# A diffusion backbone layer: row tiles of the modulation scaled on ScalarE and added up in SBUF by transfers, transposes emitted later

## The chip, the core and the metric

The kernel runs on one core of a Trainium2 chip. The metric is device time in microseconds (us). Three runs of the kernel before took 2056.44, 2061.23 and 2062.34 us, so the median is 2061.23.

## The reference

One layer of a hybrid diffusion backbone over 256 latent tokens and 256 context tokens, width 2048, all in float32:

- `mod = silu(c) @ w_mod + b_mod` gives six vectors of 2048: shift, scale and gate for the mixer (parts 0, 1, 2) and for the ConvFFN (parts 3, 4, 5). The context's own vector `c_ctx` needs parts 0 and 1 only.
- `h = rms_norm(x) * g * (1 + scale) + shift`, then one input projection `h @ w_in` (2048 x 13344) feeds windowed attention (16 query heads, 4 key heads, QK-norm, rotary, sinks, context keys) and a gated linear attention (GLA, 4 heads, both directions).
- Both are projected to 2048, weighted by sigmoid gates, added, projected again, and `x = x + gate * y`.
- ConvFFN: `h2 @ w_up` (2048 x 11264), a depthwise convolution of width 3, `silu(a) * g`, `@ w_down`, and `x = x + gate * y`. Only the latent stream is returned.

## The kernel before, in words

**The arithmetic.** Each float32 matrix is taken as two float32r halves: `hi` is a rounded copy made on ScalarE (L61), `lo` the rest, made on VectorE (L62). A product is then three on TensorE: hi by hi, hi by lo, lo by hi (L163 to L165, L186 to L189).

**Chunks.** Weights stream in chunks of two row tiles by 512 columns, 512 KB, loaded by SyncE's queue into four `raw` buffers (L68, `wload`, L137), split into three pairs `whi`, `wlo` (`wsplit`, L143). `proj_nat` (L152) sums 12 products of 512 columns into each of two or four PSUM banks' tiles for a chunk, `proj_T` (L169) does the same with the weights as the stationary side. Over a whole row range of 2048 there are 8 chunks. At the end `evac` takes the banks.

**Background.** Before each chunk `tick` (L124) may emit a step of `beside` (the generator of the GLA's or the attention's own work) and of the list `bg_steps`, at paces set in the program: so many steps a chunk. A Tile scheduler then orders each engine's instructions; an engine runs its own list strictly in order, and a transfer waits on the queue of the engine that issues it.

**The modulation.** Parts 0 and 1 are made on TensorE at the start, in five groups of row tiles, between loads of the tokens (`mod_both`, L196). Parts 3, 4, 2 and 5 belong to the latent stream alone and are background (`mod_latent`, L225): 128 steps, each loading a 256 x 512 piece of `w_mod` into one of the four `raw` buffers and doing two VectorE instructions `macc = raw * ccol + macc` over 128x512 (L237, L239). After 16 row tiles, `macc` is summed over the partitions (transposed in 32x32 blocks, reduced, one small product, L243 to L254). The paces are 0.7 a chunk beside the GLA, 2.0 beside the keys and values, 0 beside the queries, 0.5 after.

**Stages in order.** Start: tokens, parts 0 and 1, and for each group of row tiles its share of the first four projections. Then the low-rank decay input (L433), GLA heads 0 to 3 beside the other key and value projections, keys and values of attention (KA, VA), four query blocks with attention beside the next (L702), the gated GLA output (RB, L784), the merge (GA, attn_o, GB, gla_o for four column blocks, L799 to L823), the output projection (L838), then up and down projections of the ConvFFN in two halves.

**Transposes.** Results that must become a stationary side are transposed on TensorE against `ident`, four 128x128 products each, directly in `evac`: `ptk` (L680) after the key norm, `ptq` (L696), `pto` (L779, `to_T`) for the gated output and the merge, `ptx1` (L846).

**Queues.** SyncE issues the weights; GpSimd issues small parameters (`lm`, `wtm`, `wlr`, L408 to L426, the attention mask, L638), clears the GLA's `segs` (L466) and adds `gc` (L482).

Of the kernel before, what the change touches and what calls it, by code (L numbers as in the profile page):

```python
# [8 lines left out]
F32 = mybir.dt.float32  # L9
# [7 lines left out]
P = 128  # L17
D = 2048
# [12 lines left out]
def layer_kernel(ctx, tc, A, out):  # L31
# [16 lines left out]
    F2_BUFS = {"fa": 4, "fb": 4, "fc": 6, "mod": 2}  # L48
# [53 lines left out]
    def columns(name, parts, eng=G):  # L102
        rows = W2("mod", "rows", [P, P])
# [48 lines left out]
    def proj_nat(w, r0, c0, kts, lhs, evac):  # L152
        """out[token, feature] for 512 features; lhs[tile](kt) -> (hi, lo) [K, 128]"""
# [15 lines left out]
    def proj_T(w, c0, kts, rhs, evac):  # L169
        """out[feature, token] for 512 features; rhs: list of f(kt) -> (hi, lo) [K, 256]"""  # L170
# [25 lines left out]
    def mod_both(part, t0, n, dst):  # L196
        """steps for c and c_ctx on the tensor engine; dst[p, c, kt] for kt = t0..t0+n-1"""
# [27 lines left out]
    def mod_latent(part, j, dst):  # L225
        """steps for c alone: products summed over the row tiles on the vector engine"""
        a = []
        c0 = part * D + j * 512

        def step(k0):  # L230
            if k0 == 0:
                a.append(W2("mod", "macc", [P, 512]))
            raw = wload(w_mod[k0 * P:k0 * P + 256, c0:c0 + 512])
            for k in range(2):
                kt = k0 + k
                if kt == 0:
                    V.tensor_scalar(a[0], raw[:, 0, :], ccol[:, 0:1], None, op0=ALU.mult)  # L237
                else:
                    V.scalar_tensor_tensor(a[0], raw[:, k, :], ccol[:, kt:kt + 1], a[0],  # L239
                                           op0=ALU.mult, op1=ALU.add)  # L240
            if k0 == KT - 2:
                tr = W2("mod", "mtr", [P, 16, 32])
                V.transpose(tr.rearrange("p a c -> p (a c)"), a[0])  # L243
                rs = sm.tile([P, 16], F32, name="mrs", tag="mrs", bufs=2)
                V.tensor_reduce(rs, tr, op=ALU.add, axis=AX.X)
                pc = bank("pcl", (32, 16))
                PE.matmul(pc, sel[:, 0:32], rs, start=True, stop=True)
                pv = pc.rearrange("p (a b) -> p b a", b=4)
                d = dst[:, 4 * j:4 * j + 4]
                for b4 in range(4):  # L250
                    V.tensor_copy(d[32 * b4:32 * b4 + 32, :], pv[:, b4, :])
                b0 = part * 16 + j * 4
                V.tensor_tensor(d, d, bmod[:, b0:b0 + 4], op=ALU.add)

        return [lambda k0=k0: step(k0) for k0 in range(0, KT, 2)]
# [20 lines left out]
    def rms_scale(ss, n, shape):  # L276
        """(ss / n + eps) ** -0.5: exp(-ln / 2) with a Newton step"""
# [12 lines left out]
    def token_rows(tag, name, cols):  # L290
        """one factor a token, [P, 1] per tile of tokens, as a row in every partition"""
# [51 lines left out]
    def affine_split(hi, lo, xk, row, scale, shift):  # L343
        """halves of xk * row * scale + shift; xk is overwritten"""
# [12 lines left out]
    # with each part of h, that part of the sums of four projections  # L357
# [102 lines left out]
    def gla_A(h, kb, qb, res):  # L460
# [81 lines left out]
        # context keys: decay to the end (forward) or to the start (backward) of the context  # L542
# [110 lines left out]
    def norm_rope(b, r, t):  # L653
        """normalise four heads of 128 and rotate; returns [P, 4, 128] in SBUF"""
# [21 lines left out]
    def ka_evac(i, b):  # L676
        z = norm_rope(b, rk if i < 2 else None, i % 2)
        pt = bank("ptk", (P, 4, P))
        for h in range(4):
            PE.transpose(pt[:, h, :], z[:, h, :], ident)  # L680
        split(kTh[:, :, i * P:(i + 1) * P], kTl[:, :, i * P:(i + 1) * P], pt)

    bg_rate[0] = 2.0
# [5 lines left out]
    def qa_block(g):  # L689
        qT = M("qT", [P, 2, 4, T], F32R)  # L690

        def evac(t, b):
            z = norm_rope(b, rq, t)
            pt = bank("ptq", (P, 4, P))
            for h in range(4):
                PE.transpose(pt[:, h, :], z[:, h, :], ident)  # L696
            split(qT[:, 0, :, t * P:(t + 1) * P], qT[:, 1, :, t * P:(t + 1) * P], pt)
# [63 lines left out]
    for g in range(4):  # L761
        beside[:] = [attend(g, qTs), 0.8, 0.0]
# [6 lines left out]
    bg_rate[0] = 0.5  # L769
# [13 lines left out]
    for j in range(4):  # L783
        def rb_evac(t, b, j=j):  # L784
# [5 lines left out]
            to_T(s_, gh, gl, j, t)  # L790
# [11 lines left out]
    for j in range(4):  # L802
# [15 lines left out]
        def mg_evac(t, b, j=j, a1=a1, a2=a2):  # L818
            V.tensor_tensor(a2[t], b, a2[t], op=ALU.mult)
            V.tensor_tensor(a2[t], a2[t], a1[t], op=ALU.add)  # L820
            to_T(a2[t], mh, ml, j, t)
# [7 lines left out]
    while bg_steps:  # L829
        bg_steps.pop(0)()  # L830
# [6 lines left out]
    for j in range(4):  # L837
        def wo_evac(t, b, j=j):  # L838
# [5 lines left out]
            pt = bank("ptx1", (P, 4, P), side=True)  # L844
            for k in range(4):
                PE.transpose(pt[:, k, :], x1[t][:, j * 512 + k * P:j * 512 + (k + 1) * P], ident)  # L846
            dst = x1T[j // 2][:, (j % 2) * 4:(j % 2) * 4 + 4, t * P:(t + 1) * P]
            S.activation(dst, pt, AF.Copy)
# [109 lines left out]
```

## Time and profile before

| what | value |
|---|---|
| median of three runs | 2061.23 us |
| profiled execution, its span | 2061.8 us |
| instructions | 30115 |
| HBM read | 409.63 MB |
| queue of SyncE | 406.89 MB, 63.3% of 16 DMA engines' span |
| queue of GpSimd | 4.74 MB, 0.8% |

No other time of the profiled execution is listed; its span stands among the three runs. In the rows of the profile `out<-in` gives the tiles, `x` a count; a group's row ends with its busy time, the mean of one in ns, and the idle time of its engine just before it with what ended it. A stretch's row begins with its ends in us.

### The profile page before, as it was taken

The numbers are of one execution on the slowest core, as the hardware profiler recorded it, in microseconds if no ns is written. First come the engines' busy times: TensorE is split into PE (matmuls) and PEld (weight loads), VectorE is DVE, ScalarE is ACT, GpSimd is POOL, SyncE is SP. The second block draws the span as 40 slices with busy tenths as digits, with TensorE's granted clock in tenths as the row PEclk, the third lists the DMA queues.
The fourth block names the chain that finished last, engine by engine and source line by source line (L and its number), as shares of the span: only waits on it lengthen the run. The fifth ranks groups of instructions, "written<-read, shape, count | busy, mean of one in ns | idle before, by whom it ended". The sixth has DMA issues, their size and how long they took to land.

```text
span 2061.8 us, 30115 instructions
## 1 busy us (share of the span) xinstructions
PE 1999.2 (97%) x11792; PEld 1721.8 (84%) x11792; DVE 1405.7 (68%) x2149; ACT 937.4 (45%) x1306; POOL 41.9 (2%) x62
## 2 busy tenths in 40 slices
PE   6899999999999999999999999899999999999999
PEld 4679888888787777777787788899999889999987
DVE  4666778978867888777767665666666555666654
ACT  3323464552346665443334344554455334445533
POOL 0001100001000000000000000000000000000000
PEclk8999999999999999999999999999999999999999
DMA  9976434347664466787888875566666566666664
GB/s 347 337 247 197 120 111 123 113 118 226 213 186 114 121 194 192 254 270 260 264 279 272 294 235 184 164 184 184 184 183 184 194 193 187 184 184 183 183 209 150
DMA packets 214350, 413.71 MB, mean 201 GB/s; under 512 B 12548, under 2 KB 21092, under 8 KB 213184
## 3 DMA queue, kind: packets, MB, share of 16 engines
q1 hardware_dynamic: 212320, 406.89, 63.3%
q0 software_dynamic: 1360, 4.74, 0.8%
q8 instruction: 92, 1.51, 0.3%
q14 instruction: 50, 0.41, 0.1%
q10 hardware_dynamic: 528, 0.17, 0.0%
HBM read 409.63 MB, written 2.11 MB: 200 GB/s over the span
## 4 chain that ended last, share of the span: by engine, by line
PE 60%; issue 18%; DMA 11%; DVE 8%; ACT 2%; POOL 0%; DVEq 0%; ACTq 0%; POOLq 0%
PE acc L189 10%; PE acc L186 10%; PE acc L188 10%; PE acc L165 8%; PE acc L164 8%; PE acc L163 8%; DMA raw<-in_w_mod 8%; DVE wlo L62 3%; DVE macc L239 2%; DMA raw<-in_w_in 2%; PE pm L210 1%; PE pa L503 1%; ACT whi L61 1%; DMA raw<-in_w_gla_o 1%; PE po L589 1%
## 5 line engine op out<-in xcount | busy, mean ns | idle before, releaser
L61 ACT ACTIVATE whi<-raw 128x1024 fp32r<-128x1024 f32 x568 | 601.4, 1059 | 863.7 <-PE acc L165 366.4
L62 DVE TENSOR_TENSOR wlo<-raw,whi 128x1024 fp32r<-128x1024 f32 x568 | 693.3, 1222 | 428.3 <-ACT whi L61 422.7
L186 PE MATMUL acc<-h2h,whi 128*128 128x256 f32 x1408 | 399.5, 284 | 1.3 <-ACT h2h L346 1.3
L188 PE MATMUL acc<-h2l,whi 128*128 128x256 f32 x1408 | 399.5, 284 | 0.0
L189 PE MATMUL acc<-h2h,wlo 128*128 128x256 f32 x1408 | 399.2, 284 | 0.0
L186 PEld LDWEIGHTS acc<-h2h,whi 128*128 128x128 f32 x1408 | 271.3, 193 | 1.9 <-ACT h2h L346 1.8
L188 PEld LDWEIGHTS acc<-h2l,whi 128*128 128x128 f32 x1408 | 271.3, 193 | 0.2
L189 PEld LDWEIGHTS acc<-h2h,wlo 128*128 128x128 f32 x1408 | 271.3, 193 | 0.0
L239 DVE SCALAR_TENSOR_TENSOR macc<-raw,ccol,macc 128x512 f32<-128x512 f32 x240 | 180.6, 752 | 100.5 <-DMA raw<-in_w_mod 97.2
L163 PE MATMUL acc<-whi,h01hi 128*128 128x512 f32 x352 | 139.5, 396 | 0.9 <-ACT whi L61 0.9
L164 PE MATMUL acc<-wlo,h01hi 128*128 128x512 f32 x352 | 139.1, 395 | 1.3 <-DVE wlo L62 1.2
L163 PE MATMUL acc<-whi,h00hi 128*128 128x512 f32 x352 | 139.2, 395 | 0.0
L164 PE MATMUL acc<-wlo,h00hi 128*128 128x512 f32 x352 | 139.0, 395 | 0.2 <-DVE wlo L62 0.2
L165 PE MATMUL acc<-whi,h00lo 128*128 128x512 f32 x352 | 138.6, 394 | 0.0
L165 PE MATMUL acc<-whi,h01lo 128*128 128x512 f32 x352 | 138.2, 392 | 0.0
L163 PE MATMUL acc<-whi,ah 128*128 128x512 f32 x352 | 137.0, 389 | 0.0
L164 PE MATMUL acc<-wlo,ah 128*128 128x512 f32 x352 | 137.0, 389 | 0.0
L165 PE MATMUL acc<-whi,al 128*128 128x512 f32 x352 | 136.9, 389 | 0.0
L164 PEld LDWEIGHTS acc<-wlo,h01hi 128*128 128x128 f32 x352 | 66.4, 189 | 16.0 <-DVE wlo L62 3.2
L163 PEld LDWEIGHTS acc<-whi,h01hi 128*128 128x128 f32 x352 | 66.4, 189 | 14.3 <-ACT whi L61 1.3
L164 PEld LDWEIGHTS acc<-wlo,h00hi 128*128 128x128 f32 x352 | 66.2, 188 | 14.1 <-DVE wlo L62 1.3
L165 PEld LDWEIGHTS acc<-whi,al 128*128 128x128 f32 x352 | 66.1, 188 | 13.8
(369 smaller groups left out, 3393.2 us busy)
## 6 DMA issues: line engine op xcount, KB each, us to landing
raw<-in_w_in SPq DMA_DIRECT2D x208, 512.0 KB, 4.2
raw<-in_w_up SPq DMA_DIRECT2D x176, 512.0 KB, 3.7
raw<-in_w_mod SPq DMA_DIRECT2D x128, 512.0 KB, 3.9
raw<-in_w_down SPq DMA_DIRECT2D x88, 512.0 KB, 3.8
mraw<-in_w_mod SPq DMA_DIRECT2D x32, 1024.0 KB, 10.2
raw<-in_w_attn_o SPq DMA_DIRECT2D x32, 512.0 KB, 4.8
raw<-in_w_gla_o SPq DMA_DIRECT2D x32, 512.0 KB, 5.2
raw<-in_w_out SPq DMA_DIRECT2D x32, 512.0 KB, 3.8
```

Source lines behind the costliest of these rows:

```text
L61: S.activation(hi, src, AF.Copy)
L62: V.tensor_tensor(lo, src, hi.bitcast(F32), op=ALU.subtract)
L163: PE.matmul(banks[i], ahi, hi[:, k, :], start=(kt == kts[0]), stop=False)
L164: PE.matmul(banks[i], ahi, lo[:, k, :], start=False, stop=False)
L165: PE.matmul(banks[i], alo, hi[:, k, :], start=False, stop=(kt == kts[-1]))
L186: PE.matmul(o, whi, ahi, start=(kt == kts[0] and b == 0), stop=False, skip_group_check=True)
L188: PE.matmul(o, whi, alo, start=False, stop=False, skip_group_check=True)
L189: PE.matmul(o, wlo, ahi, start=False, stop=(kt == kts[-1]), skip_group_check=True)
L210: PE.matmul(a[0][q:q + 32, :], cS[:, kt, :], raw[:, k, :], start=(kt < 4), stop=(kt >= 12))
L239: V.scalar_tensor_tensor(a[0], raw[:, k, :], ccol[:, kt:kt + 1], a[0], op0=ALU.mult, op1=ALU.add)
L503: PE.matmul(pa[:, t, :], k2[:, dt, t * P:(t + 1) * P], q2[:, dt, tq * P:(tq + 1) * P], start=(dt == 0), stop=(dt == 1))
L589: PE.matmul(po, x_, y_[:, s, :], start=(n == 0), stop=(n == 11))
```

## The change

Every step of `mod_latent` now covers one row tile by 1024 columns (512 KB as before, 128 steps as before). The tile is loaded by GpSimd's queue into one of two buffers of its own (`mraw2`). ScalarE multiplies it in place by its column of `silu(c)` (for the first row tile, into `macc`), and GpSimd issues a transfer from `mraw2` to `macc`, SBUF to SBUF, that adds. The load for step i+2 is emitted right behind it. Part 5 is emitted beside the first half of the up projection instead of before the output projection. Transposes are put into a list and emitted one to three ticks later. The paces change, and the space reserved for GpSimd's descriptors is set to 4096.

```
-    F2_BUFS = {"fa": 4, "fb": 4, "fc": 6, "mod": 2}
+    F2_BUFS = {"fa": 4, "fb": 4, "fc": 6, "macc": 2, "mraw": 2}
...
-        rows = W2("mod", "rows", [P, P])
+        rows = sm.tile([P, P], F32, name="rows", tag="t128", bufs=2)
...
+    later = []
+    def defer(n, fn):
+        later.append([n, fn])
+    def flush():
+        while later:
+            later.pop(0)[1]()
     def tick():
+        for e in later:
+            e[0] -= 1
+        while later and later[0][0] < 0:
+            later.pop(0)[1]()
...
-    def mod_latent(part, j, dst):
...
-            raw = wload(w_mod[k0 * P:k0 * P + 256, c0:c0 + 512])
-            for k in range(2):
-                kt = k0 + k
-                if kt == 0:
-                    V.tensor_scalar(a[0], raw[:, 0, :], ccol[:, 0:1], None, op0=ALU.mult)
-                else:
-                    V.scalar_tensor_tensor(a[0], raw[:, k, :], ccol[:, kt:kt + 1], a[0],
-                                           op0=ALU.mult, op1=ALU.add)
...
+    def mod_latent(parts):
+        seq = [(part, dst, j, kt) for part, dst in parts for j in range(2) for kt in range(KT)]
+        raws, a = {}, [None]
+        def get(i):
+            if i < len(seq):
+                part, _, j, kt = seq[i]
+                c0 = part * D + j * 1024
+                raws[i] = W2("mraw", "mraw2", [P, 1024])
+                G.dma_start(raws[i], w_mod[kt * P:(kt + 1) * P, c0:c0 + 1024])
...
+        def step(i):
+            part, dst, j, kt = seq[i]
+            if i == 0:
+                get(0)
+                get(1)
+            raw = raws.pop(i)
+            if kt == 0:
+                a[0] = W2("macc", "macc", [P, 1024])
+                S.activation(a[0], raw, AF.Copy, scale=ccol[:, 0:1])
+            else:
+                S.activation(raw, raw, AF.Copy, scale=ccol[:, kt:kt + 1])
+                G.dma_start(a[0], raw, accum_op=ALU.add)
+            get(i + 2)
+            if kt == KT - 1:
+                defer(2, lambda acc=a[0]: finish(part, dst, j, acc))
...
-    for part, dst in ((3, shift2), (4, scale2), (2, gcol1), (5, gcol2)):
-        for j in range(4):
-            bg_steps.extend(mod_latent(part, j, dst))
-    bg_rate[:] = [0.7, 0.0]
+    bg_steps.extend(mod_latent(((3, shift2), (4, scale2), (2, gcol1))))
+    bg_rate[:] = [0.5, 0.0]
...
         z = norm_rope(b, rk if i < 2 else None, i % 2)
-        pt = bank("ptk", (P, 4, P))
-        for h in range(4):
-            PE.transpose(pt[:, h, :], z[:, h, :], ident)
-        split(kTh[:, :, i * P:(i + 1) * P], kTl[:, :, i * P:(i + 1) * P], pt)
-    bg_rate[0] = 2.0
+        def turn():
+            pt = bank("ptk", (P, 4, P))
...
+        defer(1 + i // 2, turn)
+    bg_rate[0] = 1.0
...
-        beside[:] = [attend(g, qTs), 0.8, 0.0]
+        beside[:] = [attend(g, qTs), 1.4, -2.9]
...
-    bg_rate[0] = 0.5
+    bg_rate[0] = 0.52
...
-            to_T(s_, gh, gl, j, t)
+            defer(1 + t, lambda: to_T(s_, gh, gl, j, t))
...
-    gate2 = rows_from_cols("gate2", gcol2)
+    bg_steps.extend(mod_latent([(5, gcol2)]))
+    bg_rate[:] = [0.36, 0.0]
...
+                   dynamic_dma_scratch_size=4096)
```

The query block's `ptq`, the merge's `to_T` and `ptx1` are deferred in the same way.

GpSimd's list at the start of the program, as the scheduler makes it; - is the kernel before, + the change. `mraw` are the two new buffers, `macc` the sum, `rows` the parameters of the convolution.

```order
-L645 DMA sink<-in_attn_sink 128x16
+L249 DMA mraw_2232<-in_w_mod 128x1024
+L249 DMA mraw_2234<-in_w_mod 128x1024
+L674 DMA sink<-in_attn_sink 128x16
+L249 DMA mraw_2238<-in_w_mod 128x1024
+L281 DMA macc<-mraw_2234 128x1024
+L249 DMA mraw_2404<-in_w_mod 128x1024
+L281 DMA macc<-mraw_2238 128x1024
+L249 DMA mraw_2570<-in_w_mod 128x1024
+L281 DMA macc<-mraw_2404 128x1024
```

The first steps, which the program text puts beside the GLA, stand at the very start, a load and an accumulate by turns; the loads of `lm`, `wtm` and `wlr` come behind 34 loads and 30 accumulates.

ScalarE's list at the same place, up to the first two weight splits. `xr` are the transposed tokens, `rrow` the tokens' factors, `h00hi` the first part of h.

```order
 L92 ACT_TABLE_LOAD
 L107 DMA rows_102<-in_g_ffn 16x128
-L319 ACTIVATE junk_120,ss0_121<-x00_81 128x2048
-L329 ACTIVATE xr0_116<-ptx_123 128x4x128
-L329 ACTIVATE xr1_117<-ptx_135 128x4x128
-L329 ACTIVATE xr0_116<-ptx_150 128x4x128
-L329 ACTIVATE xr1_117<-ptx_162 128x4x128
-L282 ACTIVATE rstd_175<-msq_174 128x2
-L283 ACTIVATE rstd_175<-rstd_175 128x2
-L298 ACTIVATE rrow0_191<-pr_184 128x256
-L346 ACTIVATE h00hi_253<-xr0_116,shift1_110 128x256 x2
+L350 ACTIVATE junk_120,ss0_121<-x00_81 128x2048
```
```order
+L360 ACTIVATE xr1_117<-ptx_135 128x4x128
+L278 ACTIVATE macc_2236<-mraw2_2232,ccol_96 128x1024
+L280 ACTIVATE mraw2_2234<-mraw2_2234,ccol_96 128x1024
+L280 ACTIVATE mraw2_2238<-mraw2_2238,ccol_96 128x1024
+L360 ACTIVATE xr0_116<-ptx_150 128x4x128
+L360 ACTIVATE xr1_117<-ptx_162 128x4x128
+L313 ACTIVATE rstd_175<-msq_174 128x2
+L314 ACTIVATE rstd_175<-rstd_175 128x2
+L280 ACTIVATE mraw2_2404<-mraw2_2404,ccol_96 128x1024
+L329 ACTIVATE rrow0_191<-pr_184 128x256
```

Scalings now stand among the first evacuations: 33 of them up to the h of the fourth group of row tiles (8 to 11), with 18 weight splits among them.

ScalarE's list in the merge, before and after a sigmoid gate (`m`) of the first column block: first the kernel before, then the change.

```order
L816 ACT_TABLE_LOAD
L816 ACTIVATE m_7765<-acc 128x512
L61 ACTIVATE whi<-raw 128x1024
L816 ACTIVATE m_7766<-acc 128x512
L61 ACTIVATE whi<-raw 128x1024 x8
```
```order
L280 ACTIVATE mraw_9160<-mraw_9160,ccol 128x1024
L853 ACT_TABLE_LOAD
L853 ACTIVATE m_7614<-acc 128x512
L61 ACTIVATE whi<-raw 128x1024
L853 ACTIVATE m_7615<-acc 128x512
L61 ACTIVATE whi<-raw 128x1024
L280 ACTIVATE mraw_9200<-mraw_9200,ccol 128x1024
L61 ACTIVATE whi<-raw 128x1024
L280 ACTIVATE mraw_9244<-mraw_9244,ccol 128x1024
L61 ACTIVATE whi<-raw 128x1024 x2
L280 ACTIVATE mraw_9284<-mraw_9284,ccol 128x1024
```

From the gated output to the second last column block of the merge, 63 scalings stand between 111 splits, one behind every one or two; part 5, which the program emits beside the up projection, is among them. Nothing of the modulation is left beside the GLA or the ConvFFN.

More of the change, by code (lines that the diff above doesn't have):

```diff
@@ L253, in step, with out @@
-                V.tensor_tensor(d, d, bmod[:, b0:b0 + 4], op=ALU.add)
-        return [lambda k0=k0: step(k0) for k0 in range(0, KT, 2)]
+                c = 8 * j + 4 * q
+                def out(rs=rs, c=c):
+                    pc = bank("pcl", (32, 16))
+                    PE.matmul(pc, sel[:, 0:32], rs, start=True, stop=True)
+                    pv = pc.rearrange("p (a b) -> p b a", b=4)
+                    d = dst[:, c:c + 4]
+                    for b4 in range(4):
+                        V.tensor_copy(d[32 * b4:32 * b4 + 32, :], pv[:, b4, :])
+                    V.tensor_tensor(d, d, bmod[:, part * 16 + c:part * 16 + c + 4], op=ALU.add)
@@ new lines, in finish @@
+                defer(1, out)
+        def step(i):
[13 more added lines that the diff above has]
+                defer(2, lambda acc=a[0]: finish(part, dst, j, acc))
@@ L257, in rows_from_cols @@
+        return [lambda i=i: step(i) for i in range(len(seq))]
     def rows_from_cols(name, col):
@@ L693, in evac, with turn @@
             z = norm_rope(b, rq, t)
[L694 to L697, printed above, removed]
+            def turn():
+                pt = bank("ptq", (P, 4, P))
+                for h in range(4):
+                    PE.transpose(pt[:, h, :], z[:, h, :], ident)
+                split(qT[:, 0, :, t * P:(t + 1) * P], qT[:, 1, :, t * P:(t + 1) * P], pt)
+            defer(2 + t, turn)
         proj_nat(w_in, 0, QA + g * 512, ALL, h_x, evac)
@@ L826, in layer_kernel @@
         S.preload_act_table_set("natural_log_exp_and_others")
-    while bg_steps:
-        bg_steps.pop(0)()
+    assert not bg_steps
     x1 = [M(f"x1_{t}", [P, D]) for t in range(2)]
```

45 lines of the change are left out of this document (22 added, 23 removed).

## The prediction

> **What bounds the kernel now.** I read the busy shares first, then the time by stage, then what the waiting engines wait for, and last the landing times of the transfers. The first line of the page gives busy time and share of each engine; the next rows give, for eight stretches of the program and one dense piece, the busy time of TensorE, its weight loads, VectorE, ScalarE and GpSimd, the granted clock, the DMA share and GB/s.
>
> ```profile
> PE 1999.2 (97%) x11792; PEld 1721.8 (84%) x11792; DVE 1405.7 (68%) x2149; ACT 937.4 (45%) x1306; POOL 41.9 (2%) x62
> ```
> ```profile
> 0.00:136.00 136.00, 111.11 (x809) 83.42 (x810) 73.87 (x168) 47.17 (x72) 2.98 (x9) 0.92 0.94 335
> 136.00:222.00 86.00, 85.81 (x602) 73.51 (x601) 55.00 (x89) 25.89 (x34) 7.68 (x13) 1.00 0.55 163
> 222.00:490.00 268.00, 262.52 (x1560) 224.46 (x1559) 222.62 (x421) 146.54 (x295) 28.51 (x35) 1.00 0.44 127
> 490.00:659.00 169.00, 164.42 (x740) 132.73 (x740) 129.35 (x239) 67.97 (x109) 0.00 (x0) 0.98 0.63 190
> 659.00:784.00 125.00, 124.95 (x586) 98.06 (x585) 106.65 (x227) 77.58 (x140) 0.00 (x0) 1.00 0.50 148
> 784.00:1121.00 337.00, 323.52 (x1431) 258.49 (x1430) 254.57 (x331) 139.54 (x152) 0.58 (x1) 0.99 0.80 258
> 1121.00:1305.00 184.00, 176.44 (x790) 142.93 (x788) 112.75 (x133) 81.71 (x97) 1.07 (x2) 0.99 0.73 237
> 1305.00:2062.00 757.00, 750.39 (x5285) 708.23 (x5285) 450.90 (x547) 350.96 (x412) 1.06 (x2) 0.99 0.62 183
> 1650.00:1700.00 50.00, 50.00 (x223) 41.39 (x222) 26.77 (x27) 20.01 (x19) 0.00 (x0) 1.00 0.60 191
> ```
>
> TensorE is the bound, 97% of the span. What can be won is its idle time. The stretch 0:136 has 25 us of it and runs at 0.94 of the DMA engines' time; the gated stage 222:490 has 5.5 us; 784:1121 (gated output and merge) has 13.5 us. Busy time flatters here: in the dense piece 223 products of 512 columns fill 50 us, 0.224 us each, so the 111 weight chunks of 784:1121, 12 products each, need 299 us. The stage's other large groups on TensorE add 5.2 + 3.9 + 2.9 us and three like the last row here, 17 in all:
>
> ```profile
> L779 PE MATMUL pto<-ident,sr 128*128 128x128 f32 x32 | 5.2, 290 | 4.0 <-DVE sr L789 3.1 <-DVE scale L856 0.8
> L779 PE MATMUL pto<-ident,m 128*128 128x128 f32 x24 | 3.9, 286 | 5.0 <-DVE m L820 5.0
> L739 PE MATMUL ptp<-ident,s 128*128 128x128 f32 x16 | 2.9, 283 | 0.3 <-DVE s L732 0.3
> L745 PE MATMUL poa<-pth,vah 128*128 128x512 f32 x4 | 1.7, 420 | 0.0
> ```
>
> That makes 316, so about 21 us can be won there; the last 757 us hold almost nothing. Who makes the splits wait in that stage is in the two groups with their idle time before them and the stage's DMA totals:
>
> ```profile
> L61 ACT ACTIVATE whi<-raw 128x1024 fp32r<-128x1024 f32 x111 | 117.8, 1061 | 178.3 <-PE acc L165 57.2 <-DMA raw<-in_w_in 48.7 <-DMA raw<-in_w_gla_o 35.9
> L239 DVE SCALAR_TENSOR_TENSOR macc<-raw,ccol,macc 128x512 f32<-128x512 f32 x103 | 77.2, 749 | 61.4 <-DMA raw<-in_w_mod 60.2
> DMA packets 44993, 87.04 MB, mean 258 GB/s; under 512 B 2664, under 2 KB 2664, under 8 KB 44974
> ```
>
> VectorE waits 60.2 us there for `w_mod` row tiles that share the four `raw` buffers with the weights, so `wlo` stands behind them. This is what the change takes out.
>
> **The change, part by part.** (1) VectorE loses the 256 products, ScalarE gains 128 scalings of 128x1024. The whole-run rows of the removed operations:
>
> ```profile
> L239 DVE SCALAR_TENSOR_TENSOR macc<-raw,ccol,macc 128x512 f32<-128x512 f32 x240 | 180.6, 752 | 100.5 <-DMA raw<-in_w_mod 97.2
> L237 DVE TENSOR_SCALAR macc<-raw,ccol 128x512 f32<-128x512 f32 x16 | 8.0, 501 | 3.9 <-DMA raw<-in_w_mod 3.8
> ```
>
> VectorE is relieved of 180.6 + 8.0 = 189 us. A scaling has the size of a `whi` split, 1.061 us, so ScalarE gains 128 x 1.061 = 136 us on 937: neither is the bound by its busy time. In 222:490 the chain passes through two waits for `w_mod` tiles, which no longer stand there, since no step does:
>
> ```profile
> 301.58 3.55 DMA raw<-in_w_mod
> 429.56 3.69 DMA raw<-in_w_mod
> ```
>
> With the issue gaps behind them I take **9 us saved**. In 1121:1305 TensorE is idle 7.6 us; no step is left there either, and I take **5 us saved**.
>
> (2) The transposes keep their number; only waits before them can go. TensorE's waits, in all, times, longest:
>
> ```profile
> PE pto L779 <- DVE m L820: 5.0, 3, 2.2
> PE ptk L680 <- DVE sq L671: 4.4, 1, 4.4
> PE pto L779 <- DVE sr L789: 3.1, 3, 1.9
> PE ptx L846 <- DVE x L842: 2.7, 2, 1.6
> ```
>
> That is 15 us at most. The first three lie in stages that, below, come to wait for something else; I count **3 us saved**.
>
> (3) The new chain. GpSimd's queue holds load, accumulate, load, accumulate. There are two `mraw2` buffers, so the load of step k+2 waits until the accumulate of step k has landed, and the accumulate of step k+1 stands behind that load. A step therefore costs at least one landing of an accumulate and one issue of a load. ScalarE's scalings stand at fixed places between the `whi` splits: where the chain is slower than those places assume, ScalarE stands at a scaling, the splits behind it wait, and TensorE with them. No row shows an accumulating transfer. The nearest rows are transfers of about its size by the same queue: the mask (512 KB) and `lm` (448 KB), each with its median time from issue to landing, the mask's issue on GpSimd, and the DMA share around each.
>
> ```profile
> att<-in_k_amask POOLq DMA_DIRECT2D x1, 512.0 KB, 3.8
> lm<-in_k_lmask POOLq DMA_DIRECT2D x1, 448.0 KB, 7.9
> ```
> ```profile
> 433.77 0.58 POOL L638 DMA_DIRECT2D att<-in_k_amask  x1
> 425.00:445.00 20.00, 19.15 (x101) 16.09 (x101) 15.67 (x30) 13.96 (x28) 4.14 (x5) 1.00 0.46 133
> 150.00:170.00 20.00, 19.81 (x160) 15.72 (x157) 11.23 (x19) 4.24 (x4) 6.60 (x11) 1.00 1.02 326
> ```
>
> So an accumulate lands in 3.8 us (DMA share 0.46) to 7.9 us (share 1.02), and a step takes 4.4 to 8.5 us with the 0.58 of an issue. The middle, 5.9 us, gives 6.5 us a step; I take 6.5 for the merge, where the share was 0.80, and shade it by share elsewhere: 7.5 at the start (0.94, between the middle and `lm`), 6.0 in the key and query stage (0.63).
>
> Where the 128 steps stand: the scheduler has put 33 of them ahead of the splits of the first 136 us, 32 beside the key, value and query projections, and 63 beside the gated output and merge, the last part's 32 among these. Counted by `whi` rows in the order, the second lot lies between the chunks that now begin at 490.52 and 658.90, the third between those at 784.07 and 1121.18. A lot of n steps holds n - 1 or, at the start, 30 accumulates and one load, 31 in all; that the first row tile of each sum needs no accumulate is left out. ScalarE's rows at these places; the first two are the last copy of the first tokens, beside which the chain begins, and the split of h before which its last step of the start stands:
>
> ```profile
> 13.87 0.60 ACT L329 ACTIVATE xr<-ptx 128x512 f32<-128x512 f32 x1 [0.32 <-PE ptx L324]
> 135.73 1.70 ACT L346 ACTIVATE h11hi<-xr,shift 128x256 fp32r<-128x256 f32 x4
> 490.52 1.06 ACT L61 ACTIVATE whi<-raw 128x1024 fp32r<-128x1024 f32 x1 [4.71 <-issue]
> 658.90 1.06 ACT L61 ACTIVATE whi<-raw 128x1024 fp32r<-128x1024 f32 x1
> 784.07 1.05 ACT L61 ACTIVATE whi<-raw 128x1024 fp32r<-128x1024 f32 x1
> 1121.18 1.06 ACT L61 ACTIVATE whi<-raw 128x1024 fp32r<-128x1024 f32 x1 [1.81 <-PE acc L165]
> ```
>
> - Start: 14 + 31 x 7.5 = 246 us to a place that is now reached at 136: **+111** (at 4.4: +15; at 8.5: +142).
> - Keys and queries: 31 x 6.0 = 186 against 168: **+18** (4.4: -4, TensorE's own idle time; 8.5: +95).
> - Merge: 62 x 6.5 = 403 against 337: **+66** (4.4: -21, the dense bound; 8.5: +190).
>
> A check by bytes. The merge's engines moved 258 GB/s at a share of 0.80, so 322 at full share. 111 chunks and 62 loads of 0.524 MB are 90.7 MB; 60 accumulates at the price of a copy make it 122.1 MB, 379 us; at twice that, for reading two operands, 153.6 MB, 477 us. At the start, 335 x 136 = 45.6 MB plus 34 loads and 30 accumulates is 79.1 MB, by 335/0.94 = 356 GB/s 222 us, or 266 at the double price. My 403 and 246 lie between these.
>
> The Trainium skill, "Collectives: The Full Stack", section "The bandwidth ceiling: the fold count and why AG ≠ RS ≠ AR", says that the adder in the DMA path costs no cycles but that the second source read halves the rate. By that rule the double price holds and the merge goes to 477 us, an estimate; no run here shows it yet.
>
> GpSimd's other work behind the chain: the masks, `wtm`, `wlr` and the `segs` clear stand behind 34 loads. `wlr` is needed 86 us after the place at 136, and by then the chain is past, so this costs nothing; were it late, TensorE would wait at the low-rank product.
>
> Sum: 111 + 18 + 66 - 9 - 5 - 3 = **+178 us**. The profiled span is 2061.8 us, beside a median of 2061.23 (2056.44 to 2062.34), so no offset is added: **2240 us**.
>
> **The rivals.**
> *Accumulates are quick (faster).* If one lands like the mask, 3.8 us, a step takes 4.4 us: +15 - 4 - 21 - 17 = -27, **2035 us**. It decides at an average step of 5.2 us, where 124 steps' intervals equal the 122 + 168 + 337 us they now lie beside plus the 17 saved. For it: the mask's row, and SBUF on both sides. Against it: the chain adds its own traffic where the share is 0.94 and 0.80 already. The Trainium skill, "DMA: Bandwidth & Descriptors", section "Anatomy of one DMA — SWDGE (gpsimd) path", fits a transfer as 2.0 us plus bytes over 436 GB/s. By that fit 512 KB takes 3.2 us and this rival would win; the mask's 3.8 and `lm`'s 7.9 are both longer.
> *Only the start pays.* At 5.4 us a step: +45 - 1 - 2 - 17 = +25, **2087 us**. The later stages were spaced for about such a step; the start was not.
> *The DMA engines are the bound.* At the double price the start ends at 266, keys and queries (37 chunks, 32 loads, 32 doubled accumulates: 70 MB at 322) take 217, the merge 477: 130 + 48 + 140 - 17 = +301, **2363 us**; with `lm`'s landing throughout, 8.5 us a step, +142 + 95 + 190 - 17 = +410, 2472.
>
> **How the numbers follow.** My forecast (2130 to 2340) gets 0.48, quick accumulates 0.16, only the start 0.16, the DMA bound 0.20. The range reaches from 2045, which leaves out most of the quick case, to 2440, which leaves out the end of the last. A measurement of this kernel tells about 0.3%, 6 us, from no change. Faster by more than that is 0.17, the quick case and a trace of the start's; within it 0.03; slower 0.80.
>
> **What would show it.** ScalarE's scaling group should have its idle time before it ended by `mraw2` loads, several us a step; the accumulates should land in some 6 us; the copy now at 135.73 should come near 246; the group of 111 splits should span some 400 us at a DMA share near 1; TensorE's idle time should sit in these two stretches while 222:490 shrinks a little. A landing of 4 us or less, or scalings that never wait, would prove the forecast wrong; a share of 1 with landings over 8 us would move it to the last rival.

## The result, and the profile after

The changed kernel takes **2556.38 us** (median of 4 runs, 2553.35 to 2563.99), the kernel before beside it 2061.78 us (4 runs, 2056.44 to 2064.63). The ratio is **1.2406, 95% interval 1.2379 to 1.2433**: slower by 24%, and outside the predicted range of 2045 to 2440. The profiled spans are 2554.8 and 2061.8 us, 493.0 us apart.

The busy row of the page after: VectorE has lost 170 us, ScalarE has gained 123, and TensorE's share has fallen from 97% to 83%.

```profile
PE 2127.8 (83%) x11792; PEld 1798.2 (70%) x11792; DVE 1235.7 (48%) x1893; ACT 1060.0 (41%) x1432; POOL 214.6 (8%) x310
```

No engine has become full; the time is lost in three stretches. The rows give busy time by engine (TensorE first), then the granted clock, the DMA share and GB/s. The stretches are cut at the `whi` splits number 0, 18, 67, 104, 133, 244 and 304; the splits that the prediction quoted at 490.52, 658.90, 784.07 and 1121.18 us are numbers 67, 104, 133 and 244.

```profile
63.00:307.00 244.00, 128.16 (x784) 98.55 (x784) 70.44 (x141) 66.52 (x88) 39.23 (x56) 0.74 0.87 251
307.00:648.00 341.00, 334.76 (x2056) 289.34 (x2057) 225.93 (x421) 172.10 (x327) 32.85 (x50) 0.99 0.30 87
648.00:916.00 268.00, 191.99 (x757) 148.95 (x756) 103.19 (x207) 99.17 (x140) 43.50 (x61) 0.83 0.77 193
1043.00:1618.00 575.00, 403.91 (x1409) 301.57 (x1408) 172.92 (x203) 192.68 (x205) 86.26 (x121) 0.83 0.80 210
1618.00:1785.00 167.00, 167.00 (x751) 137.43 (x750) 87.23 (x91) 75.53 (x87) 1.99 (x3) 1.00 0.66 215
```

TensorE waits 116 us in the first, 76 us in the third (keys, queries) and 171 us in the fourth (gated output and merge). In the second (the GLA's heads) it is 98% busy and the stretch is shorter than before. The DMA engines are below full share in all of them. ScalarE's rows at the cuts:

```profile
305.68 1.69 ACT L377 ACTIVATE h11hi<-xr,shift 128x256 fp32r<-128x256 f32 x4
648.34 1.06 ACT L61 ACTIVATE whi<-raw 128x1024 fp32r<-128x1024 f32 x1 [3.27 <-issue]
916.58 1.06 ACT L61 ACTIVATE whi<-raw 128x1024 fp32r<-128x1024 f32 x1 [5.28 <-PE acc L178]
1043.20 1.06 ACT L61 ACTIVATE whi<-raw 128x1024 fp32r<-128x1024 f32 x1
1617.91 1.04 ACT L61 ACTIVATE whi<-raw 128x1024 fp32r<-128x1024 f32 x1
1785.17 1.06 ACT L61 ACTIVATE whi<-raw 128x1024 fp32r<-128x1024 f32 x1 [1.66 <-PE acc L178]
```

The split of `h` that stood at 135.73 us is at 305.68. By the splits at the cuts the start (up to split 18) costs 167.1 us more than before, keys and queries take 268.2 us instead of 168.4 (+99.9), the merge 574.7 instead of 337.1 (+237.6); the GLA's stretch (18 to 67) is 9.3 us shorter, the output projection (244 to 304) 5.3 shorter, the rest 3.0 longer: 167.1 + 99.9 + 237.6 - 9.3 - 5.3 + 3.0 = 493.0.

Who waits for whom is in two groups of the page and the transfers' own rows (median us from issue to landing), first of the whole run, then by stretch (start, keys and queries, merge):

```profile
L280 ACT ACTIVATE mraw<-mraw,ccol 128x1024 f32<-128x1024 f32 x120 | 137.8, 1149 | 689.9 <-DMA mraw<-in_w_mod 685.8
...
L249 POOL DMA_DIRECT2D mraw<-in_w_mod x128 | 70.4, 550 | 925.9 <-DMA macc<-mraw 881.9
...
mraw<-in_w_mod POOLq DMA_DIRECT2D x128, 512.0 KB, 5.4
macc<-mraw POOLq DMA_DIRECT2D x120, 512.0 KB, 8.6
```
```profile
macc<-mraw POOLq DMA_DIRECT2D x25, 512.0 KB, 8.7
```
```profile
macc<-mraw POOLq DMA_DIRECT2D x30, 512.0 KB, 7.6
```
```profile
macc<-mraw POOLq DMA_DIRECT2D x59, 512.0 KB, 8.9
```

On average ScalarE stands 5.7 us before a scaling until a row tile is loaded, and GpSimd 6.9 us before a load until an accumulate has landed. In the page's chain of work that ended last, accumulates make 31% of the span. It is the chain that was foretold, with an accumulate of 8.6 us where about 6 was taken. GpSimd's rows show two steps; each begins with the wait for the accumulate before:

```profile
838.65 0.55 POOL L249 DMA_DIRECT2D mraw<-in_w_mod  x1 [7.88 <-DMA macc<-mraw]
839.19 0.91 POOL L281 DMA_DIRECT2D macc<-mraw  x1
847.91 0.55 POOL L249 DMA_DIRECT2D mraw<-in_w_mod  x1 [7.82 <-DMA macc<-mraw]
848.67 0.86 POOL L281 DMA_DIRECT2D macc<-mraw  x1 [0.21 <-issue]
```

From one accumulate's issue to the next this is 9.5 us. The mean over all such rows is 9.53 us in the start and 8.72 beside keys and queries; in the merge 63 scalings follow each other at a mean of 9.27 us.

### The profile page after: what moved, and what is told of

Same layout as the page of the kernel before. It is cut to its first block, busy times and chain, and to the rows that moved or that the text cites. A ratio compares the mean times of both kernels' runs of the same rounds, so it can differ in the third digit from the quotient of the medians.

```text
span 2554.8 us, 30140 instructions
## 1 busy us (share of the span) xinstructions
PE 2127.8 (83%) x11792; PEld 1798.2 (70%) x11792; DVE 1235.7 (48%) x1893; ACT 1060.0 (41%) x1432; POOL 214.6 (8%) x310
## 3 DMA queue, kind: packets, MB, share of 16 engines
q0 software_dynamic: 37072, 134.78, 22.5%
## 4 chain that ended last, share of the span: by engine, by line
PE 52%; DMA 34%; issue 8%; POOL 3%; ACT 2%; DVE 1%; ACTq 0%; POOLq 0%; DVEq 0%
DMA macc<-mraw 31%; PE acc L178 8%; PE acc L177 8%; PE acc L176 8%; PE acc L199 8%; PE acc L202 8%; PE acc L201 8%; DMA mraw<-in_w_mod 3%; POOL mraw L249 2%; PE pa L534 1%; PE po L620 1%; POOL macc L281 1%; PE pa L599 1%; PE ptp L776 0%; ACT whi L61 0%
## 5 line engine op out<-in xcount | busy, mean ns | idle before, releaser
L280 ACT ACTIVATE mraw<-mraw,ccol 128x1024 f32<-128x1024 f32 x120 | 137.8, 1149 | 689.9 <-DMA mraw<-in_w_mod 685.8
L176 PE MATMUL acc<-whi,h00hi 128*128 128x512 f32 x352 | 151.4, 430 | 46.1 <-ACT whi L61 20.0
L176 PE MATMUL acc<-whi,h01hi 128*128 128x512 f32 x352 | 151.4, 430 | 42.0 <-ACT whi L61 42.0
L177 PE MATMUL acc<-wlo,h01hi 128*128 128x512 f32 x352 | 151.9, 432 | 9.3 <-DVE wlo L62 9.3
L177 PE MATMUL acc<-wlo,h00hi 128*128 128x512 f32 x352 | 148.7, 422 | 6.5 <-DVE wlo L62 6.5
L249 POOL DMA_DIRECT2D mraw<-in_w_mod x128 | 70.4, 550 | 925.9 <-DMA macc<-mraw 881.9
L178 PE MATMUL acc<-whi,h01lo 128*128 128x512 f32 x352 | 148.1, 421 | 0.0
L178 PE MATMUL acc<-whi,h00lo 128*128 128x512 f32 x352 | 147.7, 420 | 0.0
L199 PE MATMUL acc<-h00hi,whi 128*128 128x256 f32 x128 | 44.5, 348 | 97.2 <-ACT whi L61 92.7
L176 PEld LDWEIGHTS acc<-whi,h00hi 128*128 128x128 f32 x352 | 73.1, 208 | 65.2 <-ACT whi L61 23.8
```

The lines of the kernel that those rows point to most:

```text
L176: PE.matmul(banks[i], ahi, hi[:, k, :], start=(kt == kts[0]), stop=False)
L177: PE.matmul(banks[i], ahi, lo[:, k, :], start=False, stop=False)
L178: PE.matmul(banks[i], alo, hi[:, k, :], start=False, stop=(kt == kts[-1]))
L199: PE.matmul(o, whi, ahi, start=(kt == kts[0] and b == 0), stop=False, skip_group_check=True)
L249: G.dma_start(raws[i], w_mod[kt * P:(kt + 1) * P, c0:c0 + 1024])
L280: S.activation(raw, raw, AF.Copy, scale=ccol[:, kt:kt + 1])
```

## The experiments

Experiments with one run have its time alone; the kernel before was run beside each.

### Plain transfers in place of accumulating ones

The sums are left out.

```diff
-                G.dma_start(a[0], raw, accum_op=ALU.add)
+                G.dma_start(a[0], raw)
```

> The changed kernel with plain transfers in place of the accumulating ones: the row tiles are no longer summed, everything else stays. Theory (a step is one landing and one load issue, and the landing is long because the load that was issued just before goes first): only the packets get cheaper, 327 ns to about 159 ns with 8 packets an engine, so the landing falls from 8.6 us by 1.3 us to about 7.3 us, 120 times, -160 us, about 2400 us. Rival (the price of the sum is the whole excess): the landing falls to about that of the mask, 3.8 to 5 us, a step to 4.4 to 5.6 us, and the time to 2080 to 2130 us. Rival (the bytes on the DMA engines): half of the accumulate's engine time goes, with a time of about 2300 us.

Measured: **2259.82 us**, 297 us less. The landings, and keys and queries and the merge as the windows give them:

```profile
mraw<-in_w_mod POOLq DMA_DIRECT2D x128, 512.0 KB, 4.6
macc<-mraw POOLq DMA_DIRECT2D x120, 512.0 KB, 5.3
```
```profile
597.00:799.00 202.00, 176.65 (x758) 139.72 (x758) 103.42 (x208) 99.79 (x143) 31.58 (x60) 0.95 0.78 255
924.00:1323.00 399.00, 346.79 (x1416) 268.06 (x1416) 173.30 (x203) 193.59 (x205) 63.61 (x121) 0.95 0.89 305
```

The landing falls by 3.3 us, not by the 1.3 of the theory, so in this traffic the price of the sum covers the whole excess of 8.6 over the forecast's 5.9 us; that rival's time is missed too, by 130 us. The third, by the bytes, is 40 us off in time, but has no reason for a landing of 5.3 us. ScalarE's scalings stand at the same chunks as in the change, so this run also tests the arithmetic of the prediction: from one transfer's issue to the next it takes a median 6.4 us, against the 6.5 taken for the merge, and the merge then takes 399 us against the 403 foretold, keys and queries 202 against 186. By the `whi` splits the start costs 116 us more than before, against 111, and the whole takes 2260 against 2240. The prediction had priced plain transfers, and for them its sum comes out.

The page's rows of GpSimd's queue (packets, MB, share of 16 engines' span) give the engine time itself. First the change, then the plain transfers, then a later run whose GpSimd queue holds the accumulates alone:

```profile
q0 software_dynamic: 37072, 134.78, 22.5%
```
```profile
q0 software_dynamic: 37072, 134.78, 18.2%
```
```profile
q0 software_dynamic: 18640, 67.66, 13.5%
```

22.5% of 2554.8 us less 18.2% of 2258.0 is 164 us, 1.37 us for each of 120 transfers. The third, 13.5% of its span of 2513.4 less the small transfers (0.8% of 2061.8, the queue's share in the kernel before), is 323 us, 2.69 us for each accumulate, so 1.32 for a copy: twice. The Trainium skill ("Collectives: The Full Stack", section "The bandwidth ceiling: the fold count and why AG ≠ RS ≠ AR") says of a ReduceScatter between cores that the second source read halves the rate; the trace agrees on the engine time. But 1.37 us of engine time do not make 3.3 us of landing.

### Three row tile buffers

```diff
-    F2_BUFS = {..., "macc": 2, "mraw": 2}
+    F2_BUFS = {..., "macc": 1, "mraw": 3}
```

> The changed kernel with three mraw buffers instead of two, and one macc buffer instead of two for room. The load of step k+2 then waits for the accumulate of step k-1 instead of k, so it is issued one landing earlier and is through when the next accumulate is issued. Theory (landing behind a load): the landing falls from 8.6 us to 5 to 6 us (the least seen was 4.8 us), a step from 9.2 to about 6, -3.2 us x 120 = -380 us where the chain is the bound, less some 10 us at each of eight hand-overs of the single sum: 2150 to 2280 us. Rival (the price of the sum): landing 8 us or more, only the 0.6 us load issue goes from each step, about 2480 us. Rival (the bytes): the same bytes, the same time, 2556 us.

Measured: **2460.18 us**. The landings, and GpSimd's waits for the accumulate before, into the same sum (total us, times, longest):

```profile
mraw<-in_w_mod POOLq DMA_DIRECT2D x128, 512.0 KB, 6.9
macc<-mraw POOLq DMA_DIRECT2D x120, 512.0 KB, 6.3
```
```profile
POOL macc L281 <- DMA macc<-mraw: 432.3, 79, 8.6
```

The landing falls to 6.3 us, near the theory's 5 to 6, and a step to a median 6.9 us; the time does not follow. It is near the rival's 2480, whose landing of 8 us did not come. Two reasons stand in the trace. The scheduler, which knows the buffers, has placed the scalings anew: in the merge 7 to 9 stand beside ten chunks instead of 5 or 6, beside keys and queries 25 of the 32 beside twenty chunks. There the chain sets the pace, and the chunks that have none beside them come after it at TensorE's own pace. In the merge 64 scalings follow each other at a mean of 6.96 us, 439 us in all, and 28 chunks stand behind them and take another 78. The last sum has moved into the ConvFFN, where fifteen accumulates stand; the time after the output projection is 46 us longer.

### No scaling in the start

```diff
     S.activation(lrp, pl, AF.Copy)
+    V.scalar_tensor_tensor(ccol, lrp[:, 0:KT], 0.0, ccol, op0=ALU.mult, op1=ALU.add)
```

> The changed kernel with the 16 scaling factors made to depend on the low-rank product, so that no scaling can stand in the first stages. Theory (the chain's rate against the places of its steps): the start's loss of 167 us goes, but 33 steps of 9.3 us now stand beside about 50 chunks of 5.4 us of the gated stage, 307 us beside 270 us and partly crowded (16 steps beside 12 chunks: 149 against 65 us), so some 100 us come back: 2430 to 2550 us. Rival (the early place of the steps is the main cost): 2556 - 167 = about 2390 us or less.

Measured: **2464.87 us**; the GLA's stretch, keys and queries, and the merge:

```profile
141.00:540.00 399.00, 357.26 (x2137) 302.68 (x2130) 231.03 (x427) 206.54 (x359) 76.45 (x112) 0.95 0.62 164
540.00:816.00 276.00, 193.98 (x759) 150.24 (x758) 103.44 (x208) 99.24 (x141) 43.23 (x61) 0.83 0.75 187
942.00:1527.00 585.00, 406.66 (x1413) 303.31 (x1412) 172.79 (x203) 192.90 (x205) 86.25 (x121) 0.82 0.79 207
```

The theory's range holds it. The start is back at 141 us, as before the change (-166), and the GLA's stretch, which now has 34 scalings, is 58 us longer than in the change; the other two are 7 and 10 us longer. Moving the steps away from the start saves 92 us of the 493; it is not the main cost.

### The transposes alone

The kernel before with `defer`, the five places that use it and the attention's new pace; nothing of the modulation changed. (An entry of the list with delay n goes out at tick n + 1, so two to four ticks later.)

> The kernel before with the later transposes and the new pace of the attention steps alone; the modulation with VectorE products, its order and its buffers as before. As predicted: the waits before the transposes were 15 us in all and mostly in places where TensorE has to wait for something else, -3 us: 2055 to 2061 us, within 0.5% of before. Rival (the transposes held more, since splits behind them were late too): 2025 to 2045 us. Rival (the later transposes push the splits of the next block back): 2070 us or more.

Measured: **2061.24 us, ratio 1.0001 (0.9989 to 1.0012)**. Of the four waits before transposes that the prediction listed, 15.2 us, there remain

```profile
PE ptx L869 <- DVE x L863: 2.7, 2, 1.6
PE pto L800 <- DVE m L841: 2.0, 3, 0.9
```

and the profiled span is 2058.6, 3.2 us shorter, a difference that the runs can't tell from nothing. But it is made, in the main, of two opposite ones: between the same `whi` splits the merge is 9.3 us shorter, and keys, values and queries are 6.6 longer. With the chain in place the later transposes wait longer, not shorter (in the change `pto` has waited 15.7 us for VectorE's `m`).

### Without the row tile loads, and with plain transfers as well

The first two row tiles are used again and again; 126 loads are left out, and in the second run the sums too.

```diff
-            if i < len(seq):
+            if i > 1:
+                raws[i] = raws[0, i % 2]
+            elif i < len(seq):
...
+                raws[0, i] = raws[i]
```

> The changed kernel with 126 of the 128 row tile loads left out: the first two tiles are scaled and summed again and again, so the sums are not those of the weights; every scaling and every accumulating transfer stays. Theory (an accumulate starts only when the load ahead of it in GpSimd's queue is through, and then runs at 327 ns a packet): with nothing ahead it lands in 4.8 to 5.6 us, a step takes 5.5 to 6 us, and by the sum of the prediction the time is 2090 to 2180 us. Rival (the sum itself is slow, wherever it stands): landing 8 us and more, step about 9, time 2500 us or more.

> The run without row tile loads (2341.88 us, accumulates landing in 4.6 us, a step of 5.2 us), now with plain transfers in place of the accumulating ones as well; ScalarE's order is the same. Left out: 126 of the loads and the summing. Theory (two parts of a landing: what stands ahead on the DMA engines, and the transfer's own packets, 2.7 us as a sum and 1.3 as a copy): with neither, the landing is about 2.9 us, the least that the plain copy showed, a step about 3.5 us, near the 3.4 us that 8 steps beside 10 chunks of 2.7 us give in the merge, so the chain almost stops counting: 2065 to 2130 us. Rival (scalings in ScalarE's order cost of themselves, whatever a landing takes): 2200 us or more.

Measured: **2341.88 us** and **2217.09 us**. The landings, in this order:

```profile
macc<-mraw POOLq DMA_DIRECT2D x120, 512.0 KB, 4.6
```
```profile
macc<-mraw POOLq DMA_DIRECT2D x120, 512.0 KB, 3.9
```

Without a load beside it an accumulate lands in 4.6 us, near the theory's 4.8, so 4.0 of the 8.6 us come only with the load. Plain transfers had taken away 3.3, and both changes together take 4.7: the two prices don't add up, most of each is there only beside the other. The times are not the theory's; in both runs they fall on the slow side, and in the second on the rival's: **scalings in ScalarE's order cost even where a transfer takes 3.9 us**. Again the scheduler has packed them: all 33 of the start stand beside the first ten chunks, those of the merge 7 to 9 beside ten. In the merge of the second run 63 scalings follow each other at a mean of 4.64 us, 288 us from the first to the last, and 34 chunks, before and after them, take another 99 us, about 3 us each. So the price is the steps at the chain's pace, plus the chunks that stand alone. By this working an even spread, which the prediction assumed, would be the cheapest case; no run has these landings with the change's own order.

### Loads on SyncE's queue

The late start with the row tile loads issued by SyncE.

```diff
-                G.dma_start(raws[i], w_mod[kt * P:(kt + 1) * P, c0:c0 + 1024])
+                nc.sync.dma_start(raws[i], w_mod[kt * P:(kt + 1) * P, c0:c0 + 1024])
```

> The late start (2464.87 us in its run) with the row tile loads issued by SyncE's queue instead of GpSimd's, so that GpSimd's queue holds accumulates alone; two mraw buffers as in the change, so a load still waits for an accumulate. Theory (the order within one queue makes the wait): the accumulates land in 4.8 to 5.8 us, a step takes 5.5 to 6.5 us, keys and queries some 186 to 200 us, the merge some 370 to 400 us: 2090 to 2180 us. Rival (an accumulate waits for any transfer, or its own price is the 8 us): landing near 8 us and a time of 2400 us or more. A third way: the landing falls but SyncE's weight loads stand behind waiting row tile loads, 2200 to 2350 us.

Measured: **2515.18 us**, 50 us more than the late start.

```profile
mraw<-in_w_mod SPq DMA_DIRECT2D x128, 512.0 KB, 3.9
macc<-mraw POOLq DMA_DIRECT2D x120, 512.0 KB, 8.2
```

The accumulates still land in 8.2 us, with no load in their queue. The theory, an order within GpSimd's queue, falls, and the rival's landing and time came. SyncE's rows show what this run has in common with the change: a row tile and a chunk of weights are issued within some 0.6 us of an accumulate, here ahead of the one at 805.69 us that landed 8.25 us later.

```profile
805.08 0.34 SPq L249 DMA_DIRECT2D mraw<-in_w_mod  x1
805.52 0.38 SPq L68 DMA_DIRECT2D raw<-in_w_in  x1
```

An accumulate that lands frees a buffer and so a load, and the scaling that this load releases lets the next splits go and with them the next chunk's load. The chain itself starts its rivals for the engines at the moment at which it issues its next transfer. Set against the landings of what had been issued before it and was still in flight: with one row tile and one other transfer, 46 accumulates of the change landed a median 3.0 us after the last of the others, and 32 copies of the first experiment 1.3 us after, each near its own engine time (2.69 and 1.32 us). With nothing in flight, 26 accumulates of the run without loads took a median 4.5 us in all.

The packets show where the time goes. With nothing in flight an accumulate's first packet starts a median 1.4 us after its issue; in the 46 cases of the change it is 4.7 us. One of them: the load issued at 838.65 us lands at 843.02, and the 327 ns packets of the accumulate issued at 839.19 begin at 843.99, while those of a chunk of weights issued at 839.40 run out. Why an accumulate's packets stand back, the runs don't tell; no run issues the accumulate ahead of the load.

### VectorE's products again, with row tile buffers of their own

Late start, later transposes, loads by GpSimd; the scaling and the accumulate are one VectorE instruction again, 128x1024. Then with three row tile buffers, one sum and no delay before it is finished; then also with other paces.

```diff
-                S.activation(raw, raw, AF.Copy, scale=ccol[:, kt:kt + 1])
-                G.dma_start(a[0], raw, accum_op=ALU.add)
+                V.scalar_tensor_tensor(a[0], raw, ccol[:, kt:kt + 1], a[0], op0=ALU.mult, op1=ALU.add)
```
```diff
-    F2_BUFS = {..., "macc": 2, "mraw": 2}
+    F2_BUFS = {..., "macc": 1, "mraw": 3}
...
-                defer(2, lambda acc=a[0]: finish(part, dst, j, acc))
+                finish(part, dst, j, a[0])
```
```diff
-    bg_rate[:] = [0.5, 0.0]
+    bg_rate[:] = [1.0, 0.0]
...
-    bg_rate[0] = 1.0
+    bg_rate[0] = 0.5
...
-    bg_rate[0] = 0.52
+    bg_rate[0] = 0.45
```

> The changed kernel, late start, with VectorE products of 128x1024 in place of scaling and accumulate; own mraw buffers, loads by GpSimd's queue, later transposes stay. Theory (only the accumulate chain costs): a load waits for a product of about 1.5 us instead of a landing, so the chain is never the bound; VectorE gets its 189 us back; the waits for row tiles that share the raw buffers go (9 + 5 us, and part of 21 us in the merge): 2035 to 2060 us. Rival (VectorE's products were what held the splits in the merge): 2061 us or more.

> The late VectorE products (2076.46 us) with three mraw buffers and one macc buffer, the sum finished at once. There VectorE waited 60.1 us for row tiles with two buffers; a third lets a load stand two products ahead. Theory (that wait is what holds it behind the kernel before): 2045 to 2060 us. Rival (the row tiles' own traffic beside the weights, or VectorE's products of 1.3 us ahead of the splits): 2065 to 2080 us as with two.

> The same with the steps spread more evenly: paces 1.0, 0.5 and 0.45 in place of 0.5, 1.0 and 0.52, so more of them stand beside the gated stage, whose chunks are twice as long, and fewer beside keys, queries and the merge. Theory: 3 to 10 us better than the version before it, 2040 to 2055 us. Rival (the gated stage has no room for more VectorE work): 2065 us or more.

Measured: **2076.46 us, ratio 1.0088 (1.0069 to 1.0107)**; **2070.88 us, 1.0051 (1.0034 to 1.0067)**; **2058.80 us, 0.9994 (0.9981 to 1.0007)**. The products of the three:

```profile
L280 DVE SCALAR_TENSOR_TENSOR macc<-mraw,ccol,macc 128x1024 f32<-128x1024 f32 x120 | 154.6, 1289 | 61.1 <-DMA mraw<-in_w_mod 60.1
```
```profile
L280 DVE SCALAR_TENSOR_TENSOR macc<-mraw,ccol,macc 128x1024 f32<-128x1024 f32 x120 | 154.3, 1286 | 40.5 <-DMA mraw<-in_w_mod 39.5
```
```profile
L280 DVE SCALAR_TENSOR_TENSOR macc<-mraw,ccol,macc 128x1024 f32<-128x1024 f32 x120 | 156.2, 1302 | 35.4 <-DMA mraw<-in_w_mod 34.7
```

Replacing scaling and accumulate by products takes away 388 us of the late start's 2464.87: the whole loss hung on the chain, but for a rest of under 1%. All three theories had promised a kernel faster than before. The first two miss, and their rivals' times hold; the third, 2040 to 2055, is missed by 4 us. VectorE's wait for row tiles was not what was left: a third of it went for 5.6 us, and the single runs, 2069 to 2082 and 2068 to 2074 us, overlap. The paces did more, 12 us. The last version stands level with the kernel before; where it differs by stretch, the merge is 9 us shorter and the GLA's stretch 4 longer:

```profile
141.00:495.00 354.00, 346.79 (x2141) 295.01 (x2140) 284.92 (x483) 172.38 (x325) 51.05 (x79) 1.00 0.48 153
495.00:662.00 167.00, 165.32 (x753) 132.92 (x751) 102.86 (x193) 68.57 (x109) 9.48 (x17) 1.00 0.43 137
789.00:1117.00 328.00, 316.10 (x1396) 256.63 (x1395) 248.24 (x268) 134.44 (x142) 33.84 (x64) 0.99 0.81 279
```

The shorter merge is not owed to the row tiles' own buffers. With the transposes alone, where `w_mod` still shares `raw` with the weights, it is as short. VectorE's products between 789 and 1117 us, of that run and of the last version:

```profile
L252 DVE SCALAR_TENSOR_TENSOR macc<-raw,ccol,macc 128x512 f32<-128x512 f32 x102 | 76.5, 750 | 65.1 <-DMA raw<-in_w_mod 63.8
```
```profile
L280 DVE SCALAR_TENSOR_TENSOR macc<-mraw,ccol,macc 128x1024 f32<-128x1024 f32 x60 | 76.8, 1280 | 16.7 <-DMA mraw<-in_w_mod 16.4
```

VectorE waits 63.8 us for row tiles in the one and 16.4 in the other, and both merges take 328 us. So the wait that the change was to take out had cost no time that these runs show. No version here beats the kernel before by more than a measurement can tell.

## Why the prediction was wrong, by its own steps

**Right: the mechanism and its places.** The chain of load, scaling, accumulate bounds the three stretches that were named, in the way that was named. Put the measured steps into the prediction's own formulas, 14 + 31 x 9.53 = 309, 31 x 8.72 = 270 and 62 x 9.27 = 575 us, beside 307, 268 and 575 measured. Each of these steps is a mean over its own stretch, so the match shows only that the chain runs through it without a pause, and that the loss sits in the size of a step. With plain transfers the sizes came out too, 116, 33 and 61 us beside the forecast's 111, 18 and 66.

**The small terms** were met, but not all for their reasons. In the output projection 5 us were to be saved and 5.3 were. In the GLA's stretch it was 9 and 9.3; yet in the two runs without loads, where next to no step stands there either, that stretch is only 1.7 us shorter than before, so the waits that went don't explain the 9.3 alone. For the transposes it was 3, and 3.2 in the run with them alone, there as the difference of two larger ones: that match is luck.

**Wrong: the size of a landing.** The step that failed is "So an accumulate lands in 3.8 us (DMA share 0.46) to 7.9 us (share 1.02), and a step takes 4.4 to 8.5 us". Both ends come from plain transfers. The runs show a landing of 8.6 us in its place (8.7, 7.6 and 8.9 in the three stretches), and steps of 9.53, 8.72 and 9.27 where 7.5, 6.0 and 6.5 were taken. Plain transfers among the same loads land in 5.3 us, so the term that was missing is the sum's own price, 3.3 us. The double engine time, which the prediction used for its check by bytes but left out of the landing, is 1.4 of them. The rest comes only among the transfers that the chain has just released itself (without loads the sum adds 0.7), while the prediction read the traffic from the DMA share of the stretch before, as if the chain met an average of it. The sizes: +111 was +167, +18 was +100, +66 was +238.

**The check by bytes** gave 403 us a comfortable place between 379 and 477. It bounds a stretch from below when the engines are full. They were not: 0.80 in the merge that took 575 us, which is 460 us of engine time, near the 477 of the double price. That price held, and the engines still stood idle for the other 115 us. A chain of waits can be longer than its bytes at any price, so the check could not support the upper side.

**The rivals.** The DMA rival's 8.5 us a step and 2472 us came nearest, but its cause, full engines with a share of 1, did not come. The quick accumulate is refuted by its landing: it needed 3.8 us, and no run has an accumulate under 4.5. Its time is doubtful too: even copies that land in 3.9 us leave 2217 us, in a run whose scalings the scheduler bunched more than in the change. The decision point of 5.2 us a step spreads the steps evenly, so it does not hold for such an order; for the change's own order it was not tested. The fit from the Trainium skill ("DMA: Bandwidth & Descriptors", section "Anatomy of one DMA — SWDGE (gpsimd) path") made 3.2 us of such a transfer, an estimate. The shortest copies here took 2.8 us, the shortest accumulates 4.5; with the bytes counted twice, for the two operands, the same fit would estimate 4.4. So it came near for a lone transfer, and says nothing of the 8.6 us in place.

**The range** ended at 2440, short even of the 2472 that a landing of 7.9 us throughout would give, and the landing was thought bounded by those 7.9. A bound taken from another operation is none.

## What to carry to other kernels

Price a serial chain of transfers by the landing that it will have among the transfers it triggers itself, not by a lone one of the same size or by the mean DMA share. When work moves from an engine that has room (VectorE at 68%) into transfers that depend on each other, each step pays the whole time to landing (8.6 us here, where a product took VectorE 1.3), and an engine that stands in order at such a step holds everything behind it. Ask of every background step both what it takes and how evenly the scheduler places it.

## What the runs showed of the hardware

- An accumulating transfer of 512 KB within SBUF takes 2.69 us of each DMA engine, a copy 1.32. GpSimd needs 0.9 us to issue the first and 0.53 for the second:

```profile
L281 POOL DMA_DIRECT2D macc<-mraw x120: 857/905/933, 14.1 to 1622.5; - x120
```
```profile
L281 POOL DMA_DIRECT2D macc<-mraw x120: 527/528/592, 14.2 to 1323.4; - x120
```

- With nothing else in flight it lands in 4.5 us (median of 26), a copy in 2.9 (median of 25); among loads 8.6 and 5.3. Over whole runs the sum adds 0.7 us without loads (4.6 against 3.9) and 3.3 with them.
- Where TensorE waits for the chain its granted clock falls: 0.74 in the start, 0.83 in the merge, where it was 0.99 before. The same merge products then take 404 us busy instead of 324. No run shows whether this costs time of its own, since TensorE was waiting there.
